# A two-layer hybrid decoder on one core: first input loaded feature-major, first rotations on POOL, low parts of four projections by accumulating transfers

## The chip, the cores and the metric

The kernel runs on one core of a Trainium2 chip. Its engines are TensorE (PE; PEld is its weight load), VectorE (DVE), ScalarE (ACT), GpSimd (POOL) and SyncE (SP, which here only issues transfers). The metric is the device time of one execution in microseconds (us), the median of several runs.

## The reference, cut to what matters

The input x is 256 rows (tokens) of 1024 features, in float32. Two layers follow one another. Each one does

```
h   = rmsnorm(x, g1)
mix = mixers(h @ w_in)          # w_in: 1024 x 2615
x   = x + mix @ w_out
h   = rmsnorm(x, g2)
x   = x + conv_glu(h @ w_up) @ w_down
```

and a last rmsnorm gives the output. The columns of `h @ w_in` are split among three kinds of attention: five heads with compressed, selected and windowed keys, five heads whose keys an indexer picks (eight small indexer heads, a top-64 of the scores), and six dilated heads. Queries and keys are rotated (RoPE) in their first 16 features (8 for the indexer): with x1, x2 the two halves of these, the result is x1 c - x2 s and x2 c + x1 s.

## The kernel before, in words

**Precision.** A float32 product is made of three products in the format fp32r. Each operand is split into a high part (its value rounded to fp32r) and a low part (value minus high part), and `mm3` adds high x high, high x low and low x high in PSUM (lines L201, L202, L203).

**Weights.** `weight` brings in one chunk: a transfer on SP's queue into a staging tile `st` (five buffers), a cast on ScalarE into the high half of a tile `hl` (L147, eight buffers), and a subtraction on VectorE into its low half (L149). The staging buffer is free for the next load when the subtraction is done; the `hl` buffer when TensorE has used both halves. `w_in` is cut into seven pieces of columns (`PIECES`), each loaded as four chunks of two k-blocks of 128 features.

**A projection.** `project` loads the four chunks of a piece, and for each chunk and each of the two blocks of 128 tokens makes two `mm3` (six products), into one PSUM bank per token block. It is a generator: each `yield` ends a step, and `fill(n)` takes n steps from the list `dense`, so that products fill TensorE's time while the attention runs. When a piece is complete, its `put_...` function scales the rows, rotates queries and keys (`rope`, four element-wise steps, L318, L319 and twice L325), and returns a function that turns (transposes) them on TensorE; that one is put off by `LAG` steps. The order of the pieces in `dense` is: `put_a0` (columns 0), `put_a1` (384), `put_i` (1103, the indexer), `put_b` (719), two `put_qk` (1463 and 1847), and the values of the dilated heads (2231). The norm of x is not applied to h before the product but to the rows of the product: `scales` makes the row scales from the sums of squares (POOL, L165 to L167, L258), and the first to use them is the scaling of QR in `put_a0` (L301).

**The beginning of layer 0.** x comes in as rows of tokens (`xr`), in four transfers of half a row block: the first two go ahead of everything on SP's and ScalarE's queues, the others behind the first weight chunk. `transposed` turns it on TensorE (L182, with the identity `ident`), and ScalarE and VectorE read the result from PSUM and write the high and low parts of x times the gain (L188, L189). Some idle matmuls on zeros (`idle`, L222) run before the first real ones. In layer 1 the input is turned in the same way, at the end of layer 0's MLP.

**Order.** A scheduler puts each engine's instructions in order from the program order, the dependencies and its own cost figures; `after(ins)` keeps an instruction behind another in that order. Each engine runs its instructions strictly in order, as do SP's and POOL's queues with the transfers that they issue. In the attention `compressed` (its products with `raw` are L597), `both`, `indexer_keys` (the turn of `kd` is L439) and `indexer` are interleaved with `fill` steps by hand.

Of the kernel before, what the change touches and what calls it, by code (L numbers as in the profile page):

```python
# [25 lines left out]
LAG = 3  # L26
AHEAD = 5
# [10 lines left out]
PIECES = ((0, 384), (384, 336), (1103, 360), (719, 384), (1463, 384), (1847, 384), (2231, 384))  # L38
# [35 lines left out]


@with_exitstack
def trunk(ctx, tc, x, w_in, cmp_w1, cmp_w2, w_out, w_up, w_down, final_g, gains, params, eye, consts_f, consts_b, out):
    nc = tc.nc
    V, S, G, PE = nc.vector, nc.scalar, nc.gpsimd, nc.tensor

# [20 lines left out]
    xr = keep.tile([128, 2, D], F32, name="xr")  # L101
    ident = keep.tile([128, 128], F32, name="ident")
    cola = keep.tile([128, 16], F32, name="cola")
    nc.sync.dma_start(xr[:, 0, 0:512], x[0, 0:128, 0:512])
    nc.scalar.dma_start(xr[:, 1, 0:512], x[0, 128:256, 0:512])
    nc.sync.dma_start(ident, eye)
    nc.scalar.dma_start(cola, gains)
    zero = keep.tile([128, 256], BF, name="zero")
    V.memset(zero, 0.0)
# [24 lines left out]
    def after(ins):  # L134
        return tc.issue_after(ins) if ins else nullcontext()

    def weight(src, a, n, then=None, behind=(None, None)):

        st = wst.tile([128, 1024], F32, name="st", tag="st", bufs=NST)
        hl = wst.tile([128, 2048], FR, name="hl", tag="hl", bufs=NHL)  # L140
        sv = st[:, :a * n].rearrange("p (a n) -> p a n", a=a)
        hv, lv = (hl[:, z:z + a * n].rearrange("p (a n) -> p a n", a=a) for z in (0, 1024))
        nc.sync.dma_start(st[:, :a * n], src)
        if then:
            then()
        with after(behind[0]):
            S.copy(hv, sv)  # L147
        with after(behind[1]):
            V.tensor_sub(lv, sv, hv.bitcast(F32))  # L149
        return hv, lv  # L150
# [4 lines left out]

    def w_in_chunk(i, c0, n, then=(None,) * 4, behind=(None, None)):
        w = piece(w_in[i], W_IN[c0] * D, 4 * 128, 2 * n)
        return [weight(w[h * 128:(h + 1) * 128], 2, n, then[h], behind) for h in range(4)]


    def rms(ss, name):
# [43 lines left out]
    for i in range(DEPTH):  # L205

        with ExitStack() as es:
# [8 lines left out]
            first, squares = None, [None, None]  # L216
            if i == 0:

                def idle(n):
                    b = bank("d")  # L220
                    for j in range(n):
                        PE.matmul(b[:, :256], zero[:, 0:128], zero, start=j == 0, stop=j == n - 1)  # L222

                idle(16)

                def other_half():
                    for t in range(2):
                        nc.sync.dma_start(xr[:, t, 512:D], x[0, t * 128:(t + 1) * 128, 512:D])

                ssq = new_ssq()  # L230
                hhi, hlo, hhl = act_pair()
                two = transposed(bank, xr, gain1[i], hhi, hlo, 0, 2, role="t")
                first = w_in_chunk(0, 0, 384, (other_half, None, None, lambda: nc.sync.dma_start(cf, consts_f)),
                                   [z.ins for z in two])
                transposed(bank, xr, gain1[i], hhi, hlo, 2, 2, role="s")
                idle(8)
            rstd = None
            rs8, rs16, rsh = (pj.tile([128, 2], F32, name=f"rs{j}") for j in range(3))

            def second_half(behind):  # L240

                with after(behind):
                    for k0 in (4, 6):
                        last = transposed(bank, xr, gain1[0], hhi, hlo, k0, 2, role="so"[k0 // 2 - 2])
                for t in range(2):
                    with after(last[0].ins):
                        squares[0] = sumsq(ssq, t, 0).ins
                    junk = pj.tile([128, 512], BF, name="junkv", tag="selb")
                    xs = xr[:, t, 512:D]
                    with after(last[1].ins):  # L250
                        squares[1] = V.scalar_tensor_tensor(junk, xs, 1.0, xs, op0=OP.mult, op1=OP.mult,
                                                            accum_out=ssq[:, t, 1:2]).ins

            def scales():
                nonlocal rstd
# [7 lines left out]
                    if i == 0:  # L263
                        nc.gpsimd.dma_start(cb, consts_b)

            def project(c0, n, done, wh=None, behind=(None, None), role="d"):
                wh = wh or w_in_chunk(i, c0, n, behind=behind)
                bs = [bank(role), bank(role)]
                for half in range(4):
                    for t in range(2):  # L270
                        for k in range(2):
                            kk = half * 2 + k
                            q = slice(t * 128, (t + 1) * 128)
                            newest[0] = mm3(bs[t][:, :n], hhi[kk // 4][:, kk % 4, q], hlo[kk // 4][:, kk % 4, q],
                                wh[half][0][:, k, :], wh[half][1][:, k, :], kk == 0, kk == 7)
                        yield
                for t in range(2):
                    f = done(t, bs[t])
                    if f:
                        later.append([LAG + t, f])  # L280
                yield

            dense, later, newest = [], [], [None]
# [216 lines left out]
            def put_a0(t, b):  # L500
# [2 lines left out]
                v_put(PA[:, t, 0:320], b[:, 0:320], rs8, t)  # L503
                v_put(PA[:, t, 320:512].rearrange("p (a d) -> p a d", d=64)[:, 0:3:2, :],
                      b[:, None, 320:384].to_broadcast([128, 2, 64]), rstd, t)
                rope(QR[:, :, 0], QR, 8, t, V, twice=True)

                def rest():
                    evac(qcT[:, t], turned(pairs(PA[:, t], t)))
# [14 lines left out]
            def put_a1(t, b):  # L524
# [1 line left out]
                ab = b[:, 64:320].rearrange("p (a c d) -> p a c d", a=2, c=2)  # L526
                pv = PV[:, t].rearrange("p (a c d) -> p a c d", a=2, c=2)
                a_put(pv, ab[:, :, 0:1, :].to_broadcast([128, 2, 2, 64]), rstd, t)
                rope(pv, pv, 8, t, V)
                a_put(vv[:, 0:2, t, :], ab[:, :, 1, :], rstd, t)  # L530
                S.activation(gate[:, t], b[:, 320:335], AF.Tanh, scale=rsh[:, t:t + 1])

# [14 lines left out]
            def put_qk(r, dst):  # L547
                def put(t, b):
# [484 lines left out]
def laid_out(a):  # L1033
# [12 lines left out]
    return dict(x=a["x"], w_in=w_in, cmp_w1=w1.reshape(DEPTH, 2, 128, -1), cmp_w2=w2.reshape(DEPTH, 128, -1), w_out=w_out,  # L1046
                w_up=w_up.reshape(DEPTH, DFF // 256, 2, 2, 128, 1024), w_down=a["w_down"], final_g=a["final_g"],
                gains=gains, params=params)

# [18 lines left out]
```

## Time and profile before

| | us |
|---|---|
| median of three runs | 646.86 |
| lowest, highest | 645.98, 648.66 |
| the profiled execution | 646.37 |
| its span from the first to the last instruction | 644.6 |

The span is what the profile's views show; the profiled execution is 1.77 us longer than its span. Busy time is the time in which an engine has an instruction under way; the ends of matmuls are modelled, so a TensorE that is shown as busy can still be short of its peak. A "releaser" is what ended an engine's wait.

### The profile page before, as it was taken

The page shows a single profiled execution, that of the slowest core. Times are in us where ns is not written, and L with a number is a line of the kernel's source. Part 1 is how long each engine was busy: PE and PEld are TensorE (multiplying, and loading weights), DVE is VectorE, ACT ScalarE, POOL GpSimd, SP SyncE. Part 2 cuts the span into 40 slices and gives each one's busy share as a digit, 9 for nine tenths or more (in the row PEclk, how much of TensorE's full clock was granted, in tenths as well). Part 3 has the DMA queues.
Part 4 walks back from the last instruction along what each step waited for, and adds up shares of the span by engine and source line. Part 5 has one row for each costly group of instructions (what it writes and reads, how often), then busy time and mean ns, then how long its engine had stood idle before and what let it go on. Part 6 is the DMA issues. An engine that isn't in the chain of part 4 may idle for free.

```text
span 644.6 us, 10526 instructions
## 1 busy us (share of the span) xinstructions
PE 629.3 (98%) x3706; PEld 540.3 (84%) x3706; DVE 530.5 (82%) x1166; ACT 402.3 (62%) x793; POOL 52.0 (8%) x115
## 2 busy tenths in 40 slices
PE   7989999999999999999999999999999999999995
PEld 6978897788888888888898888867888888888884
DVE  5989999769877777888787799985998878877774
ACT  6767688667555555555575676884865555555532
POOL 0322110011000000000020232000200000000002
PEclk9999999999999999999999999999999999999999
DMA  7972424237656666555456424333757566656601
GB/s 267 327 249 64 147 83 132 99 100 261 201 190 196 196 191 193 183 187 169 124 172 226 150 90 134 100 99 98 233 165 234 192 189 187 183 191 193 195 2 65
DMA packets 32500, 107.28 MB, mean 166 GB/s; under 512 B 3776, under 2 KB 4288, under 8 KB 31936
## 3 DMA queue, kind: packets, MB, share of 16 engines
q1 hardware_dynamic: 31536, 104.64, 51.0%
q0 software_dynamic: 336, 1.05, 0.5%
q10 hardware_dynamic: 576, 0.93, 0.4%
q8 instruction: 29, 0.48, 0.3%
q14 instruction: 23, 0.19, 0.1%
HBM read 105.55 MB, written 1.05 MB: 165 GB/s over the span
## 4 chain that ended last, share of the span: by engine, by line
PE 83%; DVE 8%; ACT 3%; DMA 2%; issue 2%; POOL 1%; POOLq 0%; ACTq 0%; DVEq 0%
PE bu L917 24%; PE bu L919 13%; PE bn L201 6%; PE bn L202 6%; PE bn L203 6%; PE bd L203 6%; PE bd L202 5%; PE bd L201 5%; DVE hl L149 2%; PE bt L365 2%; DMA st<-in_w_in_dram 2%; PE bs L345 1%; PE bt L334 1%; PE bo L720 1%; ACT P L354 1%
## 5 line engine op out<-in xcount | busy, mean ns | idle before, releaser
L149 DVE TENSOR_TENSOR hl<-st,hl 128x1024 fp32r<-128x1024 f32 (+3 forms) x208 | 232.1, 1121 | 53.6 <-ACT hl L147 53.2
L147 ACT CAST hl<-st 128x1024 fp32r<-128x1024 f32 (+3 forms) x208 | 200.9, 971 | 105.8 <-PE bn L203 43.7
L917 PE MATMUL bu<-ahl,hl 128*128 128x512 f32 x704 | 177.4, 392 | 0.0
L917 PEld LDWEIGHTS bu<-ahl,hl 128*128 128x128 f32 x704 | 127.2, 189 | 23.0
L919 PEld LDWEIGHTS bu<-ahl,hl 128*128 128x128 f32 x704 | 97.4, 190 | 7.6
L919 PE MATMUL bu<-ahl,hl 128*128 128x256 f32 x704 | 100.4, 283 | 0.0
L201 PE MATMUL bd<-hl,ahl 128*128 128x384 f32 (+2 forms) x256 | 92.6, 363 | 1.0 <-ACT hl L147 1.0
L202 PE MATMUL bd<-hl,ahl 128*128 128x384 f32 (+2 forms) x256 | 91.7, 358 | 0.4 <-DVE hl L149 0.4
L203 PE MATMUL bd<-hl,ahl 128*128 128x384 f32 (+2 forms) x256 | 91.0, 355 | 0.0
L201 PE MATMUL bn<-hl,h_hi 128*128 128x512 f32 x172 | 67.5, 393 | 0.1
L202 PE MATMUL bn<-hl,h_hi 128*128 128x512 f32 x172 | 67.2, 391 | 0.0
L203 PE MATMUL bn<-hl,h_lo 128*128 128x512 f32 x172 | 67.0, 389 | 0.0
L922 ACT COPY cross<-bu 128x256 f32<-128x256 f32 x88 | 32.3, 368 | 39.8 <-PE bu L919 39.3
L201 PEld LDWEIGHTS bd<-hl,ahl 128*128 128x128 f32 x256 | 48.1, 188 | 7.5 <-issue 2.2
L202 PEld LDWEIGHTS bd<-hl,ahl 128*128 128x128 f32 x256 | 48.3, 189 | 4.0 <-issue 1.1
L203 PEld LDWEIGHTS bd<-hl,ahl 128*128 128x128 f32 x256 | 48.2, 188 | 3.3 <-issue 1.0
L934 DVE SCALAR_TENSOR_TENSOR c<-a,cols,c 128x255 f32<-128x255 f32 (+1 forms) x88 | 40.2, 482 | 7.5 <-ACT c L932 6.3
L203 PEld LDWEIGHTS bn<-hl,h_lo 128*128 128x128 f32 x172 | 32.3, 188 | 7.1 <-DVE h_lo L947 0.3
L201 PEld LDWEIGHTS bn<-hl,h_hi 128*128 128x128 f32 x172 | 32.4, 188 | 6.9 <-ACT h_hi L946 0.9
L202 PEld LDWEIGHTS bn<-hl,h_hi 128*128 128x128 f32 x172 | 32.4, 188 | 5.9
L932 ACT ACTIVATE c<-a,cols 128x256 f32<-128x256 f32 x44 | 24.3, 595 | 13.8 <-DVE a L926 13.5
L923 DVE TENSOR_TENSOR sa<-bu,cross 128x256 f32<-128x256 f32 x44 | 18.4, 419 | 3.0 <-ACT cross L922 2.1
(247 smaller groups left out, 802.7 us busy)
## 6 DMA issues: line engine op xcount, KB each, us to landing
st<-in_w_up_dram SPq DMA_DIRECT2D x88, 512.0 KB, 4.2
st<-in_w_down_dram SPq DMA_DIRECT2D x44, 512.0 KB, 4.3
st<-in_w_in_dram SPq DMA_DIRECT2D x40, 384.0 KB, 3.9
st<-in_w_out_dram SPq DMA_DIRECT2D x12, 512.0 KB, 3.6
w<-in_cmp_w_dram SPq DMA_DIRECT2D x4, 1024.0 KB, 8.2
st<-in_w_in_dram SPq DMA_DIRECT2D x8, 360.0 KB, 3.4
st<-in_w_in_dram SPq DMA_DIRECT2D x8, 336.0 KB, 3.2
st<-in_w_out_dram SPq DMA_DIRECT2D x8, 256.0 KB, 2.7
```

Source lines behind the costliest of these rows:

```text
L147: S.copy(hv, sv)
L149: V.tensor_sub(lv, sv, hv.bitcast(F32))
L201: PE.matmul(b, ahi, whi, start=first, stop=False)
L202: PE.matmul(b, ahi, wlo, start=False, stop=False)
L203: return PE.matmul(b, alo, whi, start=False, stop=last)
L365: PE.transpose(b[:, j * 128:(j + 1) * 128], P[:, j * 128:(j + 1) * 128], ident)
L917: PE.matmul(o, wa, hhl[k // 4][:, k % 4].rearrange("p z t -> p (z t)"), start=k == 0, stop=False)
L919: PE.matmul(o[:, :L], wl, hhi[k // 4][:, k % 4, :], start=False, stop=k == 7)
L922: S.copy(cross, o[:, L:])
L923: V.tensor_tensor(sums[au][:, s], o[:, :L], cross, op=OP.add)
L932: S.activation(c[:, o:o + 256], a[:, o:o + 256], AF.Identity, bias=cw[3], scale=cw[2])
L934: V.scalar_tensor_tensor(c[:, o + d:o + 256], a[:, o:o + 256 - d], cw[w], c[:, o + d:o + 256], op0=OP.mult, op1=OP.add)
```

## The change

Three things are changed together.

1. In layer 0 the input is given to the kernel a second time, feature-major (`xt`, four chunks of 128 features x two blocks x 256 tokens). The high and low parts are written from these chunks in SBUF, without a transpose; the chunks are loaded on SP's queue in between the first weight chunks. The input as rows, which the sums of squares and the residual need, is loaded behind the sixth weight chunk, ident behind the fourth and the constants `cf` behind the eighth. The weights of the first two pieces are now asked for ahead of the first step, and the put-off turns of `put_a0` and `put_a1` in layer 0 come two steps and one step later. The idle matmuls are 20 at once instead of 16 and 8.
2. In layer 0 the rotations in `put_a0` and `put_a1` go from VectorE to POOL.
3. For the pieces at columns 719, 1463, 1847 and 2231, in both layers, the low part is no longer made by VectorE. ScalarE writes minus the rounded value into the low half, and a transfer issued by POOL adds the staging tile onto it in SBUF.

```diff
-    nc.sync.dma_start(xr[:, 0, 0:512], x[0, 0:128, 0:512])
-    nc.scalar.dma_start(xr[:, 1, 0:512], x[0, 128:256, 0:512])
-    nc.sync.dma_start(ident, eye)
     nc.scalar.dma_start(cola, gains)
...
+    def weight(src, a, n, then=None, behind=(None, None), summed=False):
...
             S.copy(hv, sv)
+        if summed:
+
+            S.activation(lv, sv, AF.Copy, scale=-1.0)
+            nc.gpsimd.dma_start(hl[:, 1024:1024 + a * n].bitcast(F32), st[:, :a * n], accum_op=OP.add)
+            return hv, lv
         with after(behind[1]):
             V.tensor_sub(lv, sv, hv.bitcast(F32))
...
+        return [weight(w[h * 128:(h + 1) * 128], 2, n, then[h], behind, c0 > 1103 or c0 == 719) for h in range(4)]
...
-                idle(16)
...
-                two = transposed(bank, xr, gain1[i], hhi, hlo, 0, 2, role="t")
-                first = w_in_chunk(0, 0, 384, (other_half, None, None, lambda: nc.sync.dma_start(cf, consts_f)),
-                                   [z.ins for z in two])
-                transposed(bank, xr, gain1[i], hhi, hlo, 2, 2, role="s")
-                idle(8)
+                idle(20)
+                xq = [tmp.tile([128, 2, L], F32, name="xq", tag="P", bufs=5) for _ in range(4)]
+                nc.sync.dma_start(xq[0].rearrange("p k t -> p (k t)"), xt[0])
                 ssq = new_ssq()
                 hhi, hlo, hhl = act_pair()
+                first, second = [], []
+
+                def later_loads(j):
+                    if j < 3:
+                        nc.sync.dma_start(xq[j + 1].rearrange("p k t -> p (k t)"), xt[j + 1])
+                    elif j == 3:
+                        nc.sync.dma_start(ident, eye)
+                    elif j == 5:
+                        for t in range(2):
+                            nc.sync.dma_start(xr[:, t, :], x[0, t * 128:(t + 1) * 128, :])
+                    elif j == 7:
+                        nc.sync.dma_start(cf, consts_f)
+
+                for j in range(8):
+                    if j < 4:
+                        for b in range(2):
+                            k = 2 * j + b
+                            g, h = gain1[0][:, k:k + 1], hhi[k // 4][:, k % 4, :]
+                            S.activation(h, xq[j][:, b], AF.Copy, scale=g)
+                            V.scalar_tensor_tensor(hlo[k // 4][:, k % 4, :], xq[j][:, b], g, h.bitcast(F32),
+                                                   op0=OP.mult, op1=OP.subtract)
+                    c, n = PIECES[j // 4]
+                    w = piece(w_in[0], W_IN[c] * D, 4 * 128, 2 * n)[j % 4 * 128:(j % 4 + 1) * 128]
+                    (first, second)[j // 4].append(weight(w, 2, n, partial(later_loads, j)))
...
-                rope(QR[:, :, 0], QR, 8, t, V, twice=True)
+                rope(QR[:, :, 0], QR, 8, t, V if i else G, twice=True)
...
-                rope(pv, pv, 8, t, V)
+                rope(pv, pv, 8, t, V if i else G)
...
-            dense += [project(0, 384, put_a0, first), project(384, 336, put_a1, behind=squares, role="s"),
+            dense += [project(0, 384, put_a0, first, lag=LAG + 2 * (i == 0)),
+                      project(384, 336, put_a1, second, role="s", lag=LAG + (i == 0)),
...
             if i == 0:
-                fill(1)
-                second_half(newest[0].ins)
-                scales()
-                fill(17 + AHEAD)
-            else:
-                scales()
-                fill(18 + AHEAD)
+                squares()
+            scales()
+            fill(18 + AHEAD + (i == 0))
...
+    xt = a["x"].reshape(L, 4, 2, 128).transpose(1, 3, 2, 0).reshape(4, 128, 2 * L)
```

## Rows read from the trace of the kernel before

**Rows 1.** The page's busy time of each engine and share of the span.

```profile
PE 629.3 (98%) x3706; PEld 540.3 (84%) x3706; DVE 530.5 (82%) x1166; ACT 402.3 (62%) x793; POOL 52.0 (8%) x115
```

**Rows 2.** The page's chain that ended last, shares by engine and by line.

```profile
PE 83%; DVE 8%; ACT 3%; DMA 2%; issue 2%; POOL 1%; POOLq 0%; ACTq 0%; DVEq 0%
PE bu L917 24%; PE bu L919 13%; PE bn L201 6%; PE bn L202 6%; PE bn L203 6%; PE bd L203 6%; PE bd L202 5%; PE bd L201 5%; DVE hl L149 2%; PE bt L365 2%; DMA st<-in_w_in_dram 2%; PE bs L345 1%; PE bt L334 1%; PE bo L720 1%; ACT P L354 1%
```

**Rows 3.** Busy time by stretch: engines (instructions), granted clock, DMA share, GB/s.

```profile
0.00:8.37 8.37, 5.32 (x33) 3.84 (x33) 1.65 (x8) 3.65 (x7) 0.56 (x9) 1.00 0.73 236
...
18.30:45.00 26.70, 24.61 (x210) 22.64 (x209) 24.19 (x64) 17.85 (x36) 8.57 (x16) 1.00 0.91 319
...
60.00:95.00 35.00, 34.60 (x233) 31.14 (x231) 34.31 (x136) 27.43 (x71) 5.31 (x16) 1.00 0.31 99
...
146.00:320.00 174.00, 174.00 (x923) 149.75 (x923) 144.02 (x211) 100.10 (x154) 2.22 (x8) 1.00 0.60 190
```

**Rows 4.** The same view: stretches of the four projections' weights, layers 0 and 1.

```profile
26.00:76.00 50.00, 47.55 (x359) 42.06 (x358) 45.54 (x137) 34.38 (x74) 11.44 (x25) 1.00 0.51 178
341.00:387.40 46.40, 44.54 (x319) 39.61 (x318) 40.04 (x125) 31.52 (x68) 10.46 (x21) 1.00 0.45 142
```

**Rows 5.** Chain of waits, first 20 us: start, duration, what ended it.

```profile
0.73 4.32 DMA xr<-in_x_dram
5.07 5.70 DMA st<-in_w_in_dram
```

**Rows 6.** Timeline, start of layer 0: start, us, engine, line, tiles, idle before.

```profile
7.49 0.82 ACT L147 CAST hl<-st 128x768 fp32r<-128x768 f32 x1
...
9.36 0.44 PE L202 MATMUL bd<-hl,ahl 128*128 128x384 f32 x1 [0.37 <-DVE hl L149]
...
18.15 0.33 PE L203 MATMUL bd<-hl,ahl 128*128 128x384 f32 x1
...
18.32 0.31 PE L201 MATMUL bs<-hl,ahl 128*128 128x336 f32 x1
```

**Rows 7.** Timeline, POOL, ACT and DVE around the row scales.

```profile
16.55 0.67 POOL L165 TENSOR_TENSOR rstdm<-ssq 128x2 f32<-128x2 f32 x1 [3.55 <-DVE junkv L251]
...
20.61 0.77 POOL L261 DMA_DIRECT2D cols<-in_params_dram  x1
...
19.61 1.48 ACT L301 ACTIVATE QR<-bd,rs 128x640 f32<-128x640 f32 x2 [0.90 <-POOL rs L258]
...
21.17 0.23 DVE L318 TENSOR_TENSOR rp<-QR,cf 128x80 f32<-128x80 f32 x1
...
22.23 0.35 DVE L304 TENSOR_SCALAR PA<-bd,rstd 128x128 f32<-128x128 f32 x1
```

**Rows 8.** Timeline, POOL: the indexer's rotations, row block 0 and 1.

```profile
38.79 1.00 POOL L318 TENSOR_TENSOR rp<-PI,cf 128x72 f32<-128x72 f32 x1 [9.40 <-DVE hl L149]
...
41.40 0.33 POOL L318 TENSOR_TENSOR rp<-PI,cf 128x72 f32<-128x72 f32 x1
```

**Rows 9.** Timeline, PE: two waits of layer 0 (idle before, releaser).

```profile
35.07 0.38 PE L597 MATMUL bo<-w,raw 128*32 128x128 f32 x5 [0.99 <-issue]
...
43.76 0.44 PE L439 MATMUL bt<-ident,kd 128*128 128x128 f32 x2 [1.04 <-ACT kd L436]
```

**Rows 10.** Groups by line and shape, 26 to 76 us: busy us, mean ns | idle before.

```profile
L149 DVE TENSOR_TENSOR hl<-st,hl 128x768 fp32r<-128x768 f32 x16 | 15.0, 948 | 0.2 <-ACT hl L147 0.2
...
L147 ACT CAST hl<-st 128x768 fp32r<-128x768 f32 x16 | 13.3, 832 | 5.9 <-PE bd L203 3.8 <-PE bo L597 1.2 <-DMA st<-in_w_in_dram 1.0
```

**Rows 11.** Timeline, layer 1: first cast of the fourth projection, its first product.

```profile
341.69 0.83 ACT L147 CAST hl<-st 128x768 fp32r<-128x768 f32 x1 [1.49 <-issue]
...
355.83 0.42 PE L201 MATMUL bd<-hl,ahl 128*128 128x384 f32 x1
```

**Rows 12.** DMA issues: tile, queue, count, KB each, us from issue to landing.

```profile
st<-in_w_in_dram SPq DMA_DIRECT2D x40, 384.0 KB, 3.9
...
fg<-in_final_g_dram POOLq DMA_DIRECT2D x1, 512.0 KB, 4.3
```

More of the change, by code (lines that the diff above doesn't have):

```diff
@@ L76, in trunk @@
 @with_exitstack
-def trunk(ctx, tc, x, w_in, cmp_w1, cmp_w2, w_out, w_up, w_down, final_g, gains, params, eye, consts_f, consts_b, out):
+def trunk(ctx, tc, x, xt, w_in, cmp_w1, cmp_w2, w_out, w_up, w_down, final_g, gains, params, eye, consts_f, consts_b, out):
     nc = tc.nc
@@ L135, in after @@
         return tc.issue_after(ins) if ins else nullcontext()
-    def weight(src, a, n, then=None, behind=(None, None)):
+    def weight(src, a, n, then=None, behind=(None, None), summed=False):
         st = wst.tile([128, 1024], F32, name="st", tag="st", bufs=NST)
@@ L157, in w_in_chunk @@
         w = piece(w_in[i], W_IN[c0] * D, 4 * 128, 2 * n)
-        return [weight(w[h * 128:(h + 1) * 128], 2, n, then[h], behind) for h in range(4)]
+        return [weight(w[h * 128:(h + 1) * 128], 2, n, then[h], behind, c0 > 1103 or c0 == 719) for h in range(4)]
     def rms(ss, name):
@@ L215, in trunk @@
             w2 = pj.tile([128, 2, 64], F32, name="w2")
-            first, squares = None, [None, None]
+            first = second = None
             if i == 0:
@@ L222, in idle @@
                         PE.matmul(b[:, :256], zero[:, 0:128], zero, start=j == 0, stop=j == n - 1)
-                idle(16)
-                def other_half():
-                    for t in range(2):
-                        nc.sync.dma_start(xr[:, t, 512:D], x[0, t * 128:(t + 1) * 128, 512:D])
+                idle(20)
+                xq = [tmp.tile([128, 2, L], F32, name="xq", tag="P", bufs=5) for _ in range(4)]
+                nc.sync.dma_start(xq[0].rearrange("p k t -> p (k t)"), xt[0])
                 ssq = new_ssq()
@@ L237, in trunk, with squares @@
             rstd = None
             rs8, rs16, rsh = (pj.tile([128, 2], F32, name=f"rs{j}") for j in range(3))
[L240 to L244, printed above, removed]
+            def squares():
                 for t in range(2):
-                    with after(last[0].ins):
-                        squares[0] = sumsq(ssq, t, 0).ins
+                    sumsq(ssq, t, 0)
@@ L248, in second_half @@
                     junk = pj.tile([128, 512], BF, name="junkv", tag="selb")
                     xs = xr[:, t, 512:D]
-                    with after(last[1].ins):
-                        squares[1] = V.scalar_tensor_tensor(junk, xs, 1.0, xs, op0=OP.mult, op1=OP.mult,
-                                                            accum_out=ssq[:, t, 1:2]).ins
+                    V.scalar_tensor_tensor(junk, xs, 1.0, xs, op0=OP.mult, op1=OP.mult, accum_out=ssq[:, t, 1:2])
             def scales():
@@ L264, in scales, with project @@
                         nc.gpsimd.dma_start(cb, consts_b)
-            def project(c0, n, done, wh=None, behind=(None, None), role="d"):
-                wh = wh or w_in_chunk(i, c0, n, behind=behind)
+            def project(c0, n, done, wh=None, role="d", lag=LAG):
+                wh = wh or w_in_chunk(i, c0, n)
                 bs = [bank(role), bank(role)]
@@ L279, in project @@
                     if f:
-                        later.append([LAG + t, f])
+                        later.append([lag + t, f])
                 yield
@@ L1045, in laid_out @@
     params = np.concatenate([columns(a[z]) for z in ("norm2_g", "conv_b", "cmp_pos", "conv_w")], 1)
-    return dict(x=a["x"], w_in=w_in, cmp_w1=w1.reshape(DEPTH, 2, 128, -1), cmp_w2=w2.reshape(DEPTH, 128, -1), w_out=w_out,
+    xt = a["x"].reshape(L, 4, 2, 128).transpose(1, 3, 2, 0).reshape(4, 128, 2 * L)
+    return dict(x=a["x"], xt=xt, w_in=w_in, cmp_w1=w1.reshape(DEPTH, 2, 128, -1), cmp_w2=w2.reshape(DEPTH, 128, -1), w_out=w_out,
                 w_up=w_up.reshape(DEPTH, DFF // 256, 2, 2, 128, 1024), w_down=a["w_down"], final_g=a["final_g"],
```

## The prediction

> **What bounds the kernel now.** I read the page's busy times first. TensorE is busy 98% of the span, VectorE 82%, ScalarE 62%, GpSimd 8% [rows 1]. The reader is to see that little can be won by moving work between the other engines unless TensorE waits for it. The chain that ended last says how much that is: 83% of it is TensorE, 8% VectorE, 3% ScalarE, 2% transfers; the subtraction of L149, part of which the change takes away, has 2%, about 13 us over the whole kernel [rows 2]. Third, the stretches. The MLP of layer 0 is TensorE without a gap (174.00 of 174.00), and nothing of the change touches it [rows 3]. Before the first products there are 8.37 us in which TensorE only warms up and turns the input [rows 3, 6]. From 18.3 to 45 us the transfers run at 0.91 of their engines, 319 GB/s, and VectorE at 24.2 of 26.7; from 60 to 95 us VectorE is busy 34.31 of 35.00 and the transfers only 0.31 [rows 3]. So the change works in three places with three limits: transfers at the start, VectorE in the attention, TensorE everywhere else. Granted clock is 1.00 in all of these stretches.
>
> The sum is made against the profiled execution, 646.37 us (span 644.60 and 1.77 around it); the median of the three runs is 0.49 higher.
>
> **The start.** Removed: 16 transposes of layer 0 and the wait for the identity. Added: the input once more, feature-major, four loads of 256 KB, on SP's queue between the first weight loads; ident, the whole of xr (1024 KB) and cf move behind them on the same queue, and cola becomes first on ScalarE's. What decides is the pace of the transfers, and the chain gives two points of it: the first half of xr landed at 5.05, when 584 KB had been asked for up to it (two halves of xr, ident, cola), and a weight chunk landed at 10.77, when it was 2248 KB [rows 5]. That is 291 KB per us. Afterwards two loads are 640 KB: the first input chunk and the first weights (648 KB with cola) land at 5.05 + 64/291 = 5.3. ScalarE's cast takes 0.82 [rows 6] and VectorE's subtraction 0.95 [rows 10], so the first product with a low part starts at 7.1 instead of 9.36 [rows 6]. Each later half of the projection needs 640 KB, 2.2 us, and 12 products 0.17 apart [rows 6], 2.04 us: about the same. The fourth weights land at 5.3 + 3 x 2.2 = 11.9, are split at 13.7, and the second projection starts at 15.8 instead of 18.32 [rows 6]. Gain 2.5 us. Bounds: 1.0 if the loads queue worse than they did, 3.2 if they keep 343 KB per us (319 GB/s at 0.91 busy [rows 3]).
>
> **The row scales come later.** The squares now need xr, which lies behind ten of the first loads and ident: 2568 + 64 + 2 x 336 + 1024 = 4328 KB. From 11.9 on at 343 KB per us this is 17.0. Two squares on each engine take 1.6, so POOL starts the mean at 18.6 instead of 16.55, and the first use of the scales (QR) comes at 21.7 instead of 19.61 [rows 7]: 2.1 later. Who waits? The evacuations of the first projection, the bank of the third one behind them (freed at 22.58 now [rows 7], 24.7 then), and the turns of QR and PA. TensorE has cover: the second projection runs from 15.8 to 23.0 (48 products of 0.17 x 336/384 = 0.15), its turns come two steps and one step later, and the weights of the third are there. What is left uncovered is about 0.8 us; bounds 0 and 2.5 (all of the gain).
>
> **Rotations on POOL.** Four rotations of layer 0 (two of QR, two of PV) leave VectorE, four steps of about 0.23 each [rows 7], some 3.5 us there. On POOL one step took 0.33 for the smaller indexer tile when undisturbed, and 1.00 while L149 ran on VectorE [rows 8]; so a rotation costs 1.4 to 4 us, behind three transfer issues of up to 0.77 each that follow the scales on POOL [rows 7]. The first issue now starts 1.0 after QR's scaling [rows 7], so then at 22.7; three issues make it 25.0, and QR's first rotation ends at 26.4, where VectorE's now begins at 21.17 and takes 0.9. TensorE meanwhile has the second and third projections. I charge 0.3 us, bounds 0 and 2.5. The Trainium skill's SBUF — State Buffer, section Who interferes with whom, says that a VectorE instruction with two SBUF inputs contends with a GpSimd one that reads SBUF. By that rule all steps that meet an L149 pay as the 1.00 row did, and the charge would be nearer to 2 than to 0.3; the rows bear it out (1.00 against 0.33), and it speaks against this part.
>
> **The low parts.** For four projections of each layer VectorE's subtraction (16 of 0.948 us in layer 0 [rows 10], 32 in all, 30 us) becomes a second ScalarE pass of the cast's length (0.832 each [rows 10], 13.3 per layer) and an accumulating transfer of 384 KB issued by POOL. The gain is TensorE time that now waits for VectorE. Two such waits show whole: before L597 (0.99 us, it wants raw, behind copies and subtractions on VectorE) and before L439 (1.04 us, behind POOL's slow rotation) [rows 9]. One more step of products now stands ahead of the first, and VectorE is relieved there of subtractions and of both PV rotations: I take 1.4 of these 2.0. From 60 to 95 us and in its like of layer 1 VectorE is full [rows 3] and loses four subtractions, 3.8 us; but TensorE is at 34.60 of 35.00, so I take 1.0 per layer, and charge 0.5 over both for new waits. Bounds: a gain of 7 us if VectorE set those stretches alone, a loss as the rivals give.
>
> Latency of the transfer is covered: in layer 1 the first cast of the fourth projection ends at 342.5 and its first product starts at 355.83 [rows 11], 13.3 us; the second pass (0.83) and an issue (0.77) leave 11.7 us for landing, and a 512 KB load issued by POOL took 4.3 [rows 12]. The stage tile is held that much longer, but five of them at some 12 us each still pass one per 2.4 us, and the four projections use one per 3 us (16 in 50). If that cover is gone, the next loads are late.
>
> The sum: -2.5 + 0.8 + 0.3 - 1.4 - 2.0 + 0.5 = -4.3, so 642.1 for the profiled execution and, 0.49 higher, 642.6 for the median.
>
> **Rivals.** (1) Absorbed, ScalarE and POOL become the bound. Over the stretch of these weights ScalarE is busy 34.38 of 50.0 in layer 0 and 31.52 of 46.4 in layer 1 [rows 4]; plus 13.3 that is 47.7 and 44.8, 95% and 97%, more than VectorE has there today (45.54 and 40.04 [rows 4]). Its exponentials then come later instead of VectorE's work, and POOL's rotations stand in one queue with issues that wait for ScalarE. Also cf lands at about 19.4 now, and a POOL copy that needs it, if it stands ahead of the mean, delays the scales 1.5 further. Then nothing of the -2.0 and -1.4 stays, and the start keeps 1.0 of its 2.5 - 0.8 - 0.3 = 1.4: 645.4, or 645.9 for the median (643.5 to 651 with the bounds of the scales and the rotations). For it: the shares. Against: over 60 to 95 alone ScalarE has 27.43 [rows 3], with four passes 30.8 of 35.
>
> (2) Slower: the accumulating transfer is too dear. It reads two tiles and writes one. At 343 KB per us a plain 384 KB takes 1.12 us of all engines; as two loads 2.25, 36 us per layer. Free transfer time in the stretches of rows 4 is 0.49 x 50 = 24.5 and 0.55 x 46.4 = 25.5 us [rows 4], and the cover of 11.7 adds as much again: 2.25 each is just hidden. This decides: at 3.4 (three loads' worth, 54 us per layer) some 18 us per layer are over. At 2.7, a fifth above the point, it is 7 per layer: 646.4 - 1.4 (what the start keeps) + 14 = 659. The place is TensorE before L202 with the low part of the fourth to seventh projections. For it: no row has such a transfer. Against: the long cover. The Trainium skill's Collectives: The Full Stack, section The bandwidth ceiling, says that a reducing transfer reads two sources and so runs at half a copy's rate, not slower for the add; by that it is 2.25, the last value that is hidden. No row here shows it.
>
> (3) VectorE set the attention after all: the 3.8 us of four subtractions come back in full in each layer, in place of the 1.0: 646.4 - 1.4 - 1.4 - 7.6 + 0.5 = 636.5, or 637 for the median.
>
> **Numbers.** The forecast has 0.52, with its own range 638.5 to 645.5; rival 1 has 0.28, rival 2 0.13, rival 3 0.07. The three runs spread by 0.4%, so half a per cent, 3.2 us, is what can be told from no change: faster is below 643.6. Of the forecast 0.08 lies above that, so faster 0.44 + 0.07 = 0.51, same 0.08 + 0.24 = 0.32, slower 0.13 + 0.04 of rival 1 = 0.17. The range reaches from rival 3 to rival 1's upper end, 637 to 651, and leaves out rival 2 and little else.
>
> **What would show it.** Right: first L202 near 7.1 and the second projection at 15.8; QR's scaling at 21 to 22 with no gap of over 1 us on TensorE after it; no idle TensorE at L202 for a transfer; accumulating transfers landing under 11 us after issue; VectorE under 31 of 35 between 60 and 95. Wrong: a gap of 2 us or more near 20 us (scales or QR late), ScalarE full with TensorE waiting for exponentials, POOL's rotations waiting behind issues, or L202 released by a transfer.

## The result, and the profile after

The changed kernel takes 649.93 us in the median (648.10 to 656.33, 13 runs) against 646.50 (645.90 to 648.66, 13 runs) for the kernel before: a ratio of 1.0061, with a 95% interval of 1.0044 to 1.0077 (the ratio is taken over all runs, not from the two medians). It is slower by 0.6%. The forecast of 642.6 had the sign wrong; the time lies near the upper end of its range, 651. The profiled execution took 649.93, with a span of 648.1.

The page of the changed kernel first: busy times, the two queues (packets, MB, share of the 16 engines), the chain by engine. The last fence is the row of POOL's queue in the kernel before.

```profile
PE 630.3 (97%) x3686; PEld 542.3 (84%) x3686; DVE 504.1 (78%) x1118; ACT 424.5 (65%) x825; POOL 74.9 (12%) x163
...
q1 hardware_dynamic: 31968, 105.95, 50.2%
q0 software_dynamic: 4944, 13.63, 11.3%
...
PE 87%; DMA 6%; POOL 2%; issue 2%; DVE 1%; ACT 1%; SPq 0%; POOLq 0%; ACTq 0%; DVEq 0%
```

```profile
q0 software_dynamic: 336, 1.05, 0.5%
```

VectorE lost 26 us of work and its share of the chain went from 8% to 1% [rows 1, 2], as meant. But transfers now have 6% of the chain where they had 2%. POOL's queue took 10.8% more of the 16 engines' span for 32 transfers: 0.108 x 648.1 / 32 = 2.2 us each. A plain load costs 0.502 x 648.1 / 105.95 MB, which is 1.2 us for 384 KB.

The stretches, in the form of [rows 3, 4]: stretch, length, busy us of PE, PEld, DVE, ACT, POOL, granted clock, DMA share, GB/s.

```profile
18.30:45.00 26.70, 24.99 (x213) 23.02 (x212) 18.95 (x47) 20.61 (x41) 14.67 (x35) 1.00 0.94 278
60.00:95.00 35.00, 29.95 (x194) 27.64 (x193) 22.79 (x100) 29.11 (x71) 10.99 (x23) 0.90 0.83 210
146.00:320.00 174.00, 174.00 (x928) 149.89 (x927) 144.48 (x212) 101.55 (x157) 2.08 (x8) 1.00 0.61 193
...
26.00:76.00 50.00, 49.26 (x377) 44.49 (x375) 35.40 (x120) 44.39 (x90) 24.44 (x47) 1.00 1.00 253
```

From 26 to 76 us TensorE is busier than before, 49.26 against 47.55 [rows 4], as meant. From 60 to 95 us it has 29.95 where it had 34.60 [rows 3], at a granted clock of 0.90. VectorE, which was full there, has 22.79; ScalarE has 29.11 of 35, less than full. So no engine has become the bound. The chain of waits (start, duration, what ended it) names the loss:

```profile
67.65 7.54 DMA hl<-st
75.24 6.95 DMA st<-in_w_out_dram
82.27 1.04 ACT hl L144
83.32 0.51 ACT rel L482
```

An accumulating transfer issued at 67.65 lands at 75.19. Only then is its staging tile free, and 0.05 us later SP issues the next load, of `w_out`. It lands at 82.2. ScalarE's cast of it (L144, formerly L147) stands at the head of ScalarE's queue, and `rel` of the indexer, which has nothing to do with it, behind. In all, SP's loads waited 32 times for an accumulating transfer, once for each (us in total, times, longest):

```profile
SPq L140 <- DMA hl<-st: 101.3, 32, 7.7
```

The timelines of ScalarE and TensorE and the stretches around 82 us show what this one does:

```profile
76.03 0.86 ACT L147 ACTIVATE hl<-st 128x768 fp32r<-128x768 f32 x1
82.27 1.04 ACT L144 CAST hl<-st 128x1024 fp32r<-128x1024 f32 x1 [5.38 <-DMA st<-in_w_out_dram]
83.22 0.59 ACT L482 ACTIVATE rel<-bs 128x512 f32<-128x512 f32 x1
...
78.79 0.34 PE L205 MATMUL bd<-hl,ahl 128*128 128x384 f32 x1
83.87 1.22 PE L748 MATMUL bs<-ksw,qrT 128*128 128x256 f32 x4 [4.74 <-ACT rel L482]
84.89 0.52 PE L203 MATMUL bd<-hl,ahl 128*128 128x384 f32 x1
```

```profile
79.00:84.00 5.00, 0.26 (x2) 0.13 (x1) 0.65 (x1) 1.73 (x3) 0.00 (x0) 0.79 1.07 278
84.00:88.00 4.00, 4.00 (x16) 4.00 (x17) 3.50 (x21) 3.62 (x12) 0.05 (x1) 0.50 0.95 286
```

ScalarE stands for 5.38 us, TensorE for 4.74, and afterwards TensorE runs for 4 us at a granted clock of 0.50, the lower of its levels (1.2 of 2.4 GHz). The same happens in layer 1: the cast at 358.87 waits 2.55 us for a load, and TensorE 2.35.

```profile
358.87 0.83 ACT L144 CAST hl<-st 128x768 fp32r<-128x768 f32 x1 [2.55 <-DMA st<-in_w_in_dram]
...
360.71 0.41 PE L203 MATMUL bd<-hl,ahl 128*128 128x384 f32 x1 [2.35 <-DVE hx L626]
```

The start went as forecast, and more. The second projection begins at 14.73 instead of 18.32 [rows 6], and QR is scaled at 17.29 instead of 19.61 [rows 7]; then TensorE waits 1.43 us for POOL's rotation of QR. (L203 to L205 are the products that were L201 to L203.)

```profile
6.53 0.56 PE L204 MATMUL bd<-hl,ahl 128*128 128x384 f32 x1
14.73 0.31 PE L203 MATMUL bs<-hl,ahl 128*128 128x336 f32 x1
...
17.29 0.80 ACT L315 ACTIVATE QR<-bd,rs 128x640 f32<-128x640 f32 x1 [1.01 <-POOL rs L272]
19.09 0.54 POOL L278 DMA_DIRECT2D cb<-in_consts_b_dram  x1
19.64 0.37 POOL L332 TENSOR_TENSOR rp<-QR,cf 128x80 f32<-128x80 f32 x1
20.43 2.37 DVE L151 TENSOR_TENSOR hl<-st,hl 128x720 fp32r<-128x720 f32 x1
20.53 0.65 POOL L339 TENSOR_TENSOR QR<-rp,rq 128x80 f32<-128x80 f32 x2
21.23 0.55 PE L348 MATMUL bt<-ident,QR 128*128 128x128 f32 x3 [1.43 <-POOL QR L339]
```

Theories. **Tile:** the accumulating transfer reads the staging tile, so the tile comes free some 7 us later than after VectorE's subtraction; loads are asked for late, and ScalarE's cast blocks its queue. **Traffic:** 32 transfers of 2.2 us (70 us of all engines), or ScalarE's second pass, are too much by themselves. **Rotations:** POOL's rotations, not the transfers, are the loss.

### The profile page after: what moved, and what is told of

Same layout as the page of the kernel before. It is cut to its first block, busy times and chain, and to the rows that moved or that the text cites. A ratio compares the mean times of both kernels' runs of the same rounds, so it can differ in the third digit from the quotient of the medians.

```text
span 648.1 us, 10590 instructions
## 1 busy us (share of the span) xinstructions
PE 630.3 (97%) x3686; PEld 542.3 (84%) x3686; DVE 504.1 (78%) x1118; ACT 424.5 (65%) x825; POOL 74.9 (12%) x163
## 3 DMA queue, kind: packets, MB, share of 16 engines
q1 hardware_dynamic: 31968, 105.95, 50.2%
## 4 chain that ended last, share of the span: by engine, by line
PE 87%; DMA 6%; POOL 2%; issue 2%; DVE 1%; ACT 1%; SPq 0%; POOLq 0%; ACTq 0%; DVEq 0%
PE bu L929 24%; PE bu L931 13%; PE bd L203 6%; PE bd L205 6%; PE bd L204 6%; PE bn L203 6%; PE bn L204 6%; PE bn L205 6%; PE bt L379 2%; PE bs L359 2%; DMA hl<-st 2%; PE bt L348 1%; PE bs L748 1%; DMA xr<-in_x_dram 1%; DMA st<-in_w_out_dram 1%
## 5 line engine op out<-in xcount | busy, mean ns | idle before, releaser
L144 ACT CAST hl<-st 128x1024 fp32r<-128x1024 f32 (+3 forms) x208 | 200.9, 972 | 102.7 <-PE bn L205 43.7
L151 DVE TENSOR_TENSOR hl<-st,hl 128x1024 fp32r<-128x1024 f32 (+4 forms) x176 | 204.0, 1163 | 56.1 <-ACT hl L144 55.9
L203 PE MATMUL bd<-hl,ahl 128*128 128x384 f32 (+2 forms) x256 | 94.6, 371 | 2.6 <-DVE hx L626 2.3
L204 PE MATMUL bd<-hl,ahl 128*128 128x384 f32 (+2 forms) x256 | 91.4, 357 | 0.0
L205 PE MATMUL bd<-hl,ahl 128*128 128x384 f32 (+2 forms) x256 | 91.3, 358 | 0.0
L203 PE MATMUL bn<-hl,h_hi 128*128 128x512 f32 x172 | 67.5, 392 | 0.1
L204 PE MATMUL bn<-hl,h_hi 128*128 128x512 f32 x172 | 67.2, 391 | 0.0
L205 PE MATMUL bn<-hl,h_lo 128*128 128x512 f32 x172 | 67.0, 389 | 0.0
L203 PEld LDWEIGHTS bd<-hl,ahl 128*128 128x128 f32 x256 | 48.9, 191 | 9.7 <-issue 5.1
L204 PEld LDWEIGHTS bd<-hl,ahl 128*128 128x128 f32 x256 | 49.0, 192 | 3.2 <-issue 0.5
L205 PEld LDWEIGHTS bd<-hl,ahl 128*128 128x128 f32 x256 | 48.8, 191 | 3.2 <-issue 0.5
L205 PEld LDWEIGHTS bn<-hl,h_lo 128*128 128x128 f32 x172 | 32.3, 188 | 7.2 <-DVE h_lo L959 0.3
L203 PEld LDWEIGHTS bn<-hl,h_hi 128*128 128x128 f32 x172 | 32.4, 188 | 6.9 <-ACT h_hi L958 0.9
L204 PEld LDWEIGHTS bn<-hl,h_hi 128*128 128x128 f32 x172 | 32.4, 188 | 5.9
L148 POOL DMA_DIRECT2D hl<-st x32 | 27.8, 870 | 50.4 <-ACT hl L147 24.2
```

The lines of the kernel that those rows point to most:

```text
L148: nc.gpsimd.dma_start(hl[:, 1024:1024 + a * n].bitcast(F32), st[:, :a * n], accum_op=OP.add)
L203: PE.matmul(b, ahi, whi, start=first, stop=False)
L204: PE.matmul(b, ahi, wlo, start=False, stop=False)
L205: return PE.matmul(b, alo, whi, start=False, stop=last)
```

## The experiments

The times are medians over five rounds, 4 to 13 runs each; ratios are to the kernel before in the same rounds. The last two columns are read from TensorE's timeline of the profiled execution: when layer 0's MLP begins (its first product with `w_up`), and how long layer 1 takes from its first product to that of its MLP. The profiled execution lies within 0.6 us of the median but for e4 and e5 (1.6 and 1.5 above it), e6 (2.1 below) and e9 (1.2 above). "Held" means that the accumulating transfer reads the staging tile.

| run | median us | ratio [95%] | layer 0 to | layer 1 |
|---|---|---|---|---|
| before | 646.50 | 1 | 139.28 | 128.78 |
| changed kernel, held | 649.93 | 1.0061 [1.0044, 1.0077] | 141.14 | 130.30 |
| e1 start and rotations | 647.94 | 1.0017 [1.0008, 1.0025] | 141.25 | 128.77 |
| e2 start only | 645.59 | 0.9980 [0.9972, 0.9989] | 138.20 | 128.80 |
| e3 transfers only, held | 653.93 | 1.0109 [1.0094, 1.0124] | 144.25 | 131.09 |
| e4 without the last piece's, held | 647.18 | 1.0009 [0.9994, 1.0023] | 139.13 | 131.17 |
| e5 source is the high half | 642.21 | 0.9925 [0.9908, 0.9943] | 138.92 | 126.22 |
| e6 start, two pieces' of layer 0, held | 651.00 | 1.0059 [1.0038, 1.0080] | 141.74 | 128.74 |
| e7 start, PV's rotation | 644.61 | 0.9960 [0.9946, 0.9974] | 137.38 | 128.80 |
| e8 start, rotations, loads on SP | 645.72 | 0.9980 [0.9970, 0.9990] | 138.10 | 128.80 |
| e9 all but the rotations, held | 653.52 | 1.0094 [1.0080, 1.0108] | 145.93 | 129.94 |
| e10 source is DRAM | 642.38 | 0.9933 [0.9921, 0.9945] | 137.71 | 126.30 |
| e11 e10, QR on VectorE | 649.51 | 1.0048 [1.0036, 1.0061] | 144.58 | 126.23 |
| e12 e11, columns 719 of layer 0 on VectorE | 641.11 | 0.9914 [0.9901, 0.9928] | 136.23 | 126.26 |
| e13 e3, source is DRAM | 645.29 | 0.9979 [0.9969, 0.9988] | 141.22 | 126.31 |
| e14 e13, columns 719 of layer 0 on VectorE | 642.77 | 0.9933 [0.9920, 0.9946] | 138.31 | 126.14 |

**The parts alone.** e1 leaves out the accumulating transfers (VectorE subtracts again), e2 also the rotations on POOL; e3 is the kernel before with the transfers alone; e4 is the changed kernel with them for three pieces.

```diff
-        return [weight(..., c0 > 1103 or c0 == 719) for h in range(4)]
+        return [weight(..., False) for h in range(4)]            # e1, e2
+        return [weight(..., 1103 < c0 < 2231 or c0 == 719) for h in range(4)]   # e4
-                rope(QR[:, :, 0], QR, 8, t, V if i else G, twice=True)
+                rope(QR[:, :, 0], QR, 8, t, V, twice=True)       # e2; PV likewise
```

> The changed kernel with the subtraction on VectorE again for all weights (no accumulating transfer); start and rotations as changed. Theory A (a stage tile held by its accumulating transfer makes the next load late, a cast of ScalarE waits for it with scaling and exponentials queued behind, and TensorE waits 4.9 us at 79 us): the lead of 3 to 5 us that the start has at 50 us stays, 641 to 643.5, no gap over 1.5 us on TensorE near 79 us, layer 1 takes as long as before. Theory B (the new order of the start is what costs, whatever makes the low parts): still 648 to 650.

> As the one above, and the four rotations of layer 0 on VectorE as before: the start alone. Theory A: 641 to 644, and TensorE's wait of 1.4 us for POOL's QR rotation at 19.6 us is gone. If the rotations on POOL are worth something by themselves (VectorE is full from 18 to 45 us), this is 0.5 to 1.5 slower than the one above; if they cost, as much faster.

> The kernel before with the accumulating transfers alone. Theory A: slower than before by what layers 0 and 1 lose in the changed kernel from 64 us on, 5 to 9 us, 651 to 656, with waits of ScalarE's casts for loads of 2 us or more. Theory B: 644 to 647, as VectorE is relieved of 30 us.

> The changed kernel with accumulating transfers for three projections, not for the last (columns 2231), whose stage tiles the first loads of the output weights follow. Theory A: the wait for the first output weights near 82 us goes, and 3 to 6 us with it: 643.5 to 647; layer 1 keeps its wait near 358 us. Theory B: unchanged within 1 us, 648 to 650.

e1 and e2 missed what theory A gave for them: the lead of the start does not last to the MLP, and e1 even lies close to theory B's range. Layer 1 takes as long as before in both, as theory A had it. e3 came out by theory A. e4 lies 0.2 us above theory A's range: the wait for the first output weights is gone, but a cast at 76.19 us waits 3.12 us for a load of `w_in` and TensorE then 2.11, and layer 1 keeps a wait of 2.48 us.

So the start is worth 1.2 us (645.59 against 646.79 in its rounds), though the second projection begins 3 us earlier; the rotations cost 2.35 on top (e1 less e2); the transfers cost 2.0 on top of both and 7.1 alone. In e2 TensorE's lead shrinks from 3.2 us at the second projection to 1.1 at the MLP. Two stretches of e2, and between them the one of the kernel before that the first is to be held against:

```profile
15.09:40.00 24.91, 22.96 (x197) 21.14 (x197) 20.06 (x55) 14.69 (x31) 7.64 (x19) 1.00 0.79 280
```

```profile
18.32:40.00 21.68, 20.64 (x184) 19.03 (x184) 20.77 (x55) 14.60 (x28) 5.44 (x10) 1.00 0.90 318
```

```profile
40.00:92.00 52.00, 49.78 (x326) 44.84 (x326) 49.38 (x174) 39.74 (x95) 11.49 (x26) 1.00 0.42 135
```

From 40 to 92 us VectorE is busy 49.38 of 52 us, but TensorE is no less so (49.78). Of the 2.1 us that are given back, 0.9 are idle time that TensorE gains before 40 us (1.95 against 1.04) and 0.4 such time from 40 to 92 (2.22 against 1.80). That an earlier input is waited away behind VectorE would fit, but is not shown. In e1 the rotations cost elsewhere than where TensorE first waits for them. The fourth piece begins at the same time as in e2 (38.21 and 38.08), but the order of TensorE differs by then, and at 52 us it waits for `iq`, with a lower clock after it:

```profile
53.77 1.23 PE L479 MATMUL bs<-ik,iq 128*128 128x256 f32 x4 [1.77 <-DVE iq L475]
```

```profile
52.00:56.00 4.00, 2.23 (x9) 2.23 (x9) 3.87 (x9) 1.72 (x5) 1.32 (x3) 0.63 0.21 70
56.00:60.00 4.00, 4.00 (x13) 3.72 (x13) 3.29 (x13) 1.13 (x4) 2.47 (x6) 0.52 0.31 98
```

**Is it the held tile?** e5 changes where the transfer reads from (the high half of the `hl` tile) and ScalarE's factor. All engines run the same list of instructions in the same order as in the changed kernel, and the 32 transfers have the same size. The low halves then hold 0.0005 of the weights instead of the remainder. e10 reads the weights a second time from DRAM instead, which gives the exact remainder; its order is the same too.

```diff
-            S.activation(lv, sv, AF.Copy, scale=-1.0)
-            nc.gpsimd.dma_start(hl[:, 1024:1024 + a * n].bitcast(F32), st[:, :a * n], accum_op=OP.add)
+            S.activation(lv, sv, AF.Copy, scale=-0.9995)         # e5
+            nc.gpsimd.dma_start(hl[:, 1024:1024 + a * n].bitcast(F32), hl[:, 0:a * n].bitcast(F32), accum_op=OP.add)
+            nc.gpsimd.dma_start(hl[:, 1024:1024 + a * n], src.bitcast(FR), accum_op=OP.add)   # e10, scale -1.0
```

> The changed kernel, in which the accumulating transfer adds the high half of the weight tile instead of the staging tile, so that the staging tile is free after ScalarE's two passes; the same transfers of the same size and the same passes remain, and the low halves then hold 0.0005 of the weights instead of the exact remainder (ScalarE's factor is -0.9995). Theory A (the transfer holds the staging tile, so later loads are asked for late and ScalarE's cast waits at the head of its queue for them): no cast in 60 to 90 us waits more than 1 us for a load, the 4.9 us gap on TensorE at 79 and the low clock behind it go, and the time falls from 649.9 to 645 to 647.5. Theory B (32 transfers of some 2.2 us are too much work for the transfer engines, or ScalarE's second pass is): the waits stay and the time is 649 to 651.

> The changed kernel, in which the accumulating transfer reads the weights a second time from DRAM in place of the staging tile (the low half is then the exact remainder again). Theory A (holding the staging tile is what costs): 641 to 643.5, like the run with the high half as the source. Theory B (that run was fast because its transfer read the same SBUF tile that it wrote to): 647 to 650, the extra 12.6 MB of reading on top.

642.21 and 642.38 against 649.93: the tile theory holds, and its gain is larger than I expected for e5 (645 to 647.5). The waits of ScalarE's casts for loads, in the view of waits (us in total, times, longest), first of the changed kernel, then of e5:

```profile
ACT hl L144 <- DMA st<-in_w_out_dram: 5.8, 2, 5.4
ACT hl L144 <- DMA st<-in_w_in_dram: 4.7, 6, 2.5
```

```profile
ACT hl L144 <- DMA st<-in_w_up_dram: 1.3, 3, 0.6
ACT hl L144 <- DMA st<-in_w_in_dram: 1.0, 2, 0.8
```

The traffic stays (the queue has 10.9% in e5 and 11.1% in e10), and the single transfer even takes longer to land. The issues of the changed kernel and of e10 (KB each, median us to landing), and e10's stretch 350 to 380 us:

```profile
hl<-st POOLq DMA_DIRECT2D x32, 384.0 KB, 6.4
```

```profile
hl<-in_w_in_dram POOLq DMA_DIRECT2D x32, 384.0 KB, 8.8
```

```profile
350.00:380.00 30.00, 30.00 (x210) 27.21 (x209) 21.92 (x83) 28.29 (x60) 13.90 (x26) 1.00 1.07 272
```

TensorE is at 30.00 of 30 us with a DMA share of 1.07 and ScalarE at 28.29. So neither the traffic nor ScalarE's second pass costs TensorE anything there. From 26 to 46 us of layer 0 it is another matter (e13, below).

**Does it hold in the kernel before?** e13 and e14 are e3 with DRAM as the source, e14 with VectorE subtracting for columns 719 of layer 0.

> The kernel before plus the accumulating transfers alone, reading the weights from DRAM instead of from the staging tile. Theory A (the held staging tile is what made this edit cost 7.1 us): the wait of TensorE at 41.6 us shrinks to under 2 us, layer 1 takes 126.2 in place of 131.1 us up to its MLP, and the time is 642 to 645. Theory B (the transfers' own work, or ScalarE's second pass): 651 to 654 as before.

> As the run before, with the low parts of columns 719 of layer 0 back on VectorE. If the first accumulating transfers of layer 0 come too late also with the old start: 0.5 to 2 us faster than the run before, 641.5 to 643.5. If not: the same within 0.5 us.

e13 takes 8.6 us from e3 with an unchanged order of instructions. TensorE's longest wait, first of e3, then of e13:

```profile
47.42 0.66 PE L205 MATMUL bd<-hl,ahl 128*128 128x384 f32 x1 [5.68 <-DVE hid L620]
```

```profile
44.70 0.41 PE L205 MATMUL bd<-hl,ahl 128*128 128x384 f32 x1 [2.39 <-DVE hid L620]
```

It shrank, but not under the 2 us that I had set, and 645.29 lies 0.3 us above the range. In e3 `hid` waits for ScalarE's scalings, and these stand behind two casts with idle time before them, 3.06 us for a load and then 2.44; in e13 these are 0.53 and 1.27. The view names no releaser for the second ones, but by the trace's semaphores the load of that cast landed 0.07 us before it began, in e13 at 42.79 after an ask at 31.49. Tiles are not held in e13; here the transfers themselves are late. From 26 to 46 us, first e13, then e14, the stretch and the weight loads (KB each, median us to landing):

```profile
26.00:46.00 20.00, 17.22 (x154) 15.22 (x154) 10.43 (x39) 15.66 (x31) 8.42 (x16) 0.99 1.05 318
st<-in_w_in_dram SPq DMA_DIRECT2D x9, 384.0 KB, 11.3
```

```profile
26.00:46.00 20.00, 18.58 (x170) 16.97 (x170) 15.34 (x46) 14.24 (x30) 5.70 (x12) 1.00 0.89 297
st<-in_w_in_dram SPq DMA_DIRECT2D x9, 384.0 KB, 6.1
```

In the kernel before the transfers have 0.87 of their engines there and a load lands in 4.1 us. So the traffic theory, wrong for layer 1, has its place here: with the accumulating transfers of columns 719 the transfer engines are full, without them (e14) they are not, and the time falls by 2.5 us, more than the 0.5 to 2 that I gave it. (A full share alone does not do it: e10 has 1.02 there, and its loads land in 6.3 us.)

The column of layer 1 sums up the tile theory: 128.7 to 128.8 without transfers in layer 1, 129.9 to 131.2 with held tiles, 126.1 to 126.3 with freed ones.

**The first low parts of layer 0.** Where, with the new start, QR's rotation is on VectorE and accumulating transfers make columns 719 of layer 0, the time is far above what I expected (e6, e9, e11).

> The feature-major start, all rotations on VectorE, accumulating transfers for columns 719 and 1463 of layer 0 alone. Theory A (the lead of the start is given back because VectorE sets layer 0's attention, and the transfers hurt only where staging tiles are asked for again at once): VectorE loses 7.6 us ahead of 70 us, layer 0's MLP begins 1 to 3 us earlier than at 138.2, layer 1 keeps 128.8: 642.5 to 645. Theory B (any accumulating transfer delays loads and casts more than it relieves VectorE): 646 to 649.

> The changed kernel with all rotations on VectorE (feature-major start and all accumulating transfers remain, with the staging tile as their source). Theory A (POOL's rotations cost 2.35 us by themselves, the held staging tile the rest): 647 to 648.5, with a wait of ScalarE's cast for a load of over 2 us still there. Theory B (the loss comes of POOL having both rotations and accumulating issues in one queue): 643 to 646.

> As the run before with DRAM as the source, and QR's rotation back on VectorE. If QR's rotation on POOL costs here what it cost without the accumulating transfers (3.3 us), less what VectorE-bound attention no longer takes: 638.5 to 641. If the accumulating transfers have hidden it: 641 to 643.5.

> As the run before, and the low parts of columns 719 of layer 0 back on VectorE. Theory A (the first accumulating transfers of layer 0 come too late for their products, 1.65 us of waiting at 38 us and the lower clock after it): 0.5 to 2 us faster than the run before. Theory B (that wait is given back, or VectorE's four subtractions cost as much there): within 0.5 us of it or slower.

e6, e9 and e11 missed what both theories gave. ScalarE and TensorE of e11:

```profile
30.80 0.37 ACT L373 CAST ksw<-bt 128x256 fp32r<-128x256 f32 x1 [2.75 <-DVE u L552]
31.07 0.85 ACT L147 ACTIVATE hl<-st 128x768 fp32r<-128x768 f32 x1
...
41.87 0.44 PE L204 MATMUL bd<-hl,ahl 128*128 128x384 f32 x1 [4.33 <-DMA hl<-in_w_in_dram]
```

ScalarE's second pass for the first chunk of columns 719 stands behind a cast of `ksw` that waits 2.75 us for VectorE. POOL issues the transfer at 32.23, the transfers are at 1.01 of their engines from 30 to 40 us, and the low part is there at 41.87: 4.33 us late. In e6 and e9 the same product waits 2.22 us each. In the changed kernel and in e10 QR's rotation on POOL gives TensorE another order; there that pass runs at about 29, and the product waits not at all and 0.50 us. With VectorE subtracting for this one piece (e12) the wait is gone and the time 8.4 us lower, where I had given 0.5 to 2; at 641.11 it is the fastest of all. The rotations on POOL cost 2.35 us without transfers and save 3.6 with them (e9 less the changed kernel): the parts don't add. That they save by the other order, which spares TensorE this wait, fits, but no run takes that gain apart.

**QR's rotation.** e7 has QR's rotation on VectorE and PV's on POOL, e8 has both on POOL, and the three loads of constants on SP's queue; neither has accumulating transfers.

```diff
-                        nc.gpsimd.dma_start(cols, params)        # e8; w2 of layer 0 and cb likewise
+                        nc.sync.dma_start(cols, params)
```

> The feature-major start, QR's rotation on VectorE, PV's on POOL, no accumulating transfers. Theory A (of the 2.35 us that both rotations on POOL cost, QR's is the cause: it stands behind three issues on POOL): 645.3 to 646.3. Theory B (PV's is: it moves VectorE's and TensorE's order at 50 us, where a 1.8 us gap and a lower clock follow): 647 to 648.5, with p193 (the first product of the fifth projection) near 54.8.

> The feature-major start, both rotations on POOL, no accumulating transfers, and the three loads of constants behind the scales issued by SP instead of POOL in layer 0. Theory A (POOL's three issues ahead of QR's rotation are what costs): the 1.8 us wait of TensorE at 20 us for QR goes and the time falls from 647.9 to 645.3 to 646.5. Theory B (that wait is given back anyway; the loss is later): the wait goes and the time stays at 647.3 to 648.5.

e8 came out by theory A; e7 is 0.7 us faster than theory A gave. PV's rotation on POOL gains 1.0 (e7 less e2), QR's costs 3.3 (e1 less e7), and 2.2 of these go when POOL's three issues no longer stand ahead of it (e8 less e1). TensorE's wait for QR shrinks from 1.54 to 0.65 us.

## Why the prediction was wrong

**The step that failed** is the last one of "the low parts": "five of them at some 12 us each still pass one per 2.4 us". From a cast to the next cast out of the same tile it took 12.3 us at layer 1's wait (346.58 to 358.87) and 16.9 at layer 0's (65.36 to 82.27: two passes 2.0, the transfer 7.8, the next load 7.0), so the 12 was right at one place and short at the other. What failed at both is to hold one per 2.4 us against an average need of one per 3: ScalarE takes chunks in bursts, five of them one per 2.5 us from 65.36 to 75.30, and one per 1.9 us from 346.58 to 354.15. The sixth cast then waits at the head of ScalarE's queue. I named what is late then, "the next loads", but worked out no price for it; the 0.5 us charged stood for all new waits together. The rival that ended on the slow side had nearly the right price (2.25 us, measured 2.2), but its place was the low part at TensorE (L202, now L204) and its point of decision 3.4 us; in the changed kernel no L204 waits for a transfer, and the loss comes through the staging tile, SP's queue and ScalarE's queue. (In e11 one does, 4.33 us.) Rival 1's range, 643.5 to 651, holds the time, but not for its reason: ScalarE is busy 44.39 of 50 us and not 47.7, and it stands idle for 5.38 us just where TensorE waits for it. The sum lost 7.6 us by this (649.93 less e10's 642.38), more than the whole error of 7.3.

**Point by point.** The start: -2.5 was forecast for the second projection; it came 3.6 us earlier, but only 1.2 reached the end (e2): 2.1 of the lead are given back before the MLP, by waits and an order of TensorE that I had not charged to the start. The scales: +0.8 was forecast for QR at 21.7; xr landed at 14.6 instead of 17.0, and QR came at 17.29, so the term is 0. The rotations: +0.3 was forecast, 2.35 measured (e1), inside the bounds of 0 to 2.5, and at a place that I had not looked at. The Trainium skill, SBUF — State Buffer, section Who interferes with whom, has a VectorE instruction with two SBUF inputs contend with a GpSimd one that reads SBUF. The trace agrees: a subtraction beside QR's rotation took 2.37 us where others of its shape take 0.90. But that need not be what the rotations cost: 2.2 of QR's 3.3 us go with the three issues ahead of it (e8). The two waits: both are gone (L609 and L453, formerly L597 and L439), worth up to the 1.4 that I took. VectorE's relief: -1.0 per layer was forecast; with the tile freed layer 1 gains 2.5 (128.8 to 126.3), with the tile held it loses 1.5. The price of a transfer: the Trainium skill, Collectives: The Full Stack, section The bandwidth ceiling, has a reducing transfer at half a copy's rate. Measured were 2.2 us against 1.2, 1.8 times, so this nearly agrees.

With the tile freed, as the sum took it to be, the change comes out at 642.38 (e10), 0.2 from 642.6. Part of that is luck. The start gave 1.2 instead of 2.5 - 0.8 = 1.7, the rotations cost 2.35 instead of 0.3, and the low parts gained 5.6 (647.94 of e1 less 642.38) instead of 1.4 + 2.0 - 0.5 = 2.9: errors that cancel.

**Left open.** How much of what layer 0 of e13 (141.22) loses against the kernel before (139.28) is the full transfer engines, and how much ScalarE's second passes, is not taken apart further than by e14, which removes it. What gives the lead of the start back is not shown. More staging buffers, the other way to pass loads earlier, were not tried.

## What to carry to other kernels

When work moves from an engine to a transfer, count how long its source buffer stays taken: the engine gave the tile back after 1 us, the transfer after 7, and the next load of a ring of five paid. Then look at who waits for that load in an in-order queue: the cast at the head of ScalarE's queue stopped exponentials and scalings that needed nothing of it. Reading the source from DRAM a second time freed the tile and cost no more than the SBUF source that holds nothing (642.38 against 642.21). Where the transfers are nearly full already, here from 26 to 46 us of layer 0, the work was better left on VectorE (e12, e14).

## What was not expected of the hardware

An accumulating transfer of 384 KB took 2.2 us of all 16 engines from SBUF and 2.1 from DRAM (0.106 x 640.7 / 32 in e10): the source made no difference. Waits of 1.77 (e1) and 4.74 us (the changed kernel) on TensorE were each followed by some 4 us at a granted clock of 0.52 and 0.50; after the 2.22 and 2.00 us of e6 it stayed at 1.00, and after e9's wait for the same product, 2.22 us as well, it was 0.57 from 44 to 48 us:

```profile
44.00:48.00 4.00, 4.00 (x19) 3.96 (x18) 2.37 (x6) 3.57 (x6) 0.85 (x1) 0.57 1.05 204
```

A short wait can cost more than its length, but not every one does. A subtraction on VectorE beside a GpSimd rotation took 2.37 us instead of 0.90, so it is VectorE that pays too; PV's two last steps on POOL, beside two subtractions of 1.78 together, took 1.81 instead of 0.46:

```profile
27.19 1.78 DVE L151 TENSOR_TENSOR hl<-st,hl 128x720 fp32r<-128x720 f32 x2
27.27 1.81 POOL L339 TENSOR_TENSOR PV<-rp,rq 128x32 f32<-128x32 f32 x2
...
29.71 0.46 POOL L339 TENSOR_TENSOR PV<-rp,rq 128x32 f32<-128x32 f32 x2
```
